# Which token tiles are gathered and which go through the dense expert pass: tiles 0, 3, 6, 7 against tiles 0, 5, 6, 7, with other token steps

## The chip, the cores and the metric

The kernel runs on one core of a Trainium2 chip. The metric is the device time of the whole program in microseconds (us), as the median of several runs. The kernel before takes 3573.17 us (three runs, 3567.7 to 3573.94). The execution that the profiler recorded took 3550.3 us, and its span, from the first to the last instruction, is 3548.6 us.

## What is computed

One decoder block over 1024 tokens of width 1024, in float32. Cut to what matters here:

```python
u = modulate(rmsnorm(x, norm_mix_g), sh_mix, sc_mix)
p = u @ w_in
mix = concat([conformer_conv(p[:, :1024]), rwkv7_mix(p[:, 1024:])]) @ w_out   # rwkv7: a scan over the tokens
x = x + gt_mix * mix
u = modulate(rmsnorm(x, norm_ffn_g), sh_ffn, sc_ffn)
# PEER: per token 8 heads, each with the best 16 of 128 x 128 experts
q = u @ w_q ; s = q . sub_keys ; best 16 of 256 candidates -> expert[t, h, k], gate = softmax(best)
h = gelu(sum_d expert_u[expert[t, h, k]] * u[t])
x = x + gt_ffn * sum_{h,k} gate * h * expert_v[expert[t, h, k]]
out = rmsnorm(x, final_g)
```

Each token uses 128 experts (8 heads, 16 each) of 16384. One expert is one row of `expert_u` and one of `expert_v`, 4 KB each.

## The kernel before

The 1024 tokens are eight tiles of 128. There are two ways to compute the experts of a tile.

- **Gathered** tiles (`GATHER`). For each of the tile's 128 selected experts per token, POOL issues one indirect DMA that brings, for all 128 tokens, the expert's row of u and v: 128 x 2048 floats, 1 MB, into one of three buffers `row` (`ROWS = 3`, `stream_fetch`). VectorE forms the dot product of the row's first half with the token (`stream_use`, result `hj`), ScalarE applies gelu and the gate to `hj`, and VectorE adds the second half, scaled by `hj`, to an accumulator (`stream_add`). Then the buffer is free for the next row. In the first stage a quarter of the dot products is done by POOL and ScalarE instead (`SHARE`, `stream_useg`), the operands lie in SBUF, and the accumulator is called `acc`; in the second stage the token copy `up` and the accumulator `ap` lie in PSUM.
- **Dense** tiles (all others, `DT_`). The selected experts and gates become two one-hot matrices per token (`onea`, `oneb`, `stream_g`), a matmul makes of them the token's 128 x 128 gate matrix, and this goes to DRAM (`Gd`, `stream_h`). Later one dense pass over all 16384 experts serves the four dense tiles at once (512 columns): 128 blocks of experts, each with 24 matmuls into `ph` and as many into `po`/`pC` (`stream_mm`), with loads of `w`, `v` and `gt`.

The program has two stages. In the first, these streams run side by side, each in its own order: `stream_a` (input projection, one step per entry of `MACROS`), `stream_l` and `stream_taps` (convolution), `stream_b` (the RWKV recurrence, tile after tile, strictly in sequence), `stream_c` (output projection, then the queries and the scores `s`, one step per entry of `MACROS`), `stream_d` (top 16, the selection and the gates), `stream_g` and `stream_h` (one-hots), and the gather streams. A step of `stream_c` starts its RWKV half when the recurrence has finished the last tile of the step, and `stream_d` releases a tile's experts after the scores of its whole step. The gathered tiles are fetched in the order of their numbers, one row after the other.

The first stage ends when the recurrence, the convolution and the one-hots of all dense tiles are done and `stream_c` has passed the output projection of the last step (line 1395). Then its memory is released and the second stage starts: the dense pass, the rest of `stream_c` and `stream_d`, and the gathers that are left. A tile's final norm (`tile_end`) follows its last row; the dense tiles are finished in `stream_sum`.

The order of the instructions of each engine is fixed when the program is built. A planner (`Issue.go`) picks, step by step, the operation of any stream that can start first by its own cost model. In it all transfers share one resource, and a gathered row takes 2920 ns of that (`GA`) while a 512 KB load takes 1456 ns (`LD`). On the chip each engine then follows that order and waits where an operand is late.

Lines that decide about the change:

```python
MACROS = [128, 128, 256, 256, 256]                                          # 65
GATHER = (0, 3, 6, 7)                                                       # 67
yield Wait(lambda: done["B"] >= i0 + nt - XB)                               # 572, stream_a, XB = 3
yield Wait(lambda: done["B"] >= i0 + nt)                                    # 981, stream_c
yield Wait(lambda: i in SEL and SEL[i].get("n", 0) > j)                     # 1260, stream_fetch
ROW[n] = tl(gat, [128, 2048], "row", bufs=ROWS)                             # 1261
```

Of the kernel before, what the change touches and what calls it, by code (L numbers as in the profile page):

```python
# [61 lines left out]
    _o += _w  # L62
NCOL = _o

MACROS = [128, 128, 256, 256, 256]

GATHER = (0, 3, 6, 7)
GE = 4
RUN_EXPERTS = True

# [212 lines left out]
def block_kernel(ctx, tc, xT, cols, ada_w, w_in, w0, w2a2, g2, w_out, w_q, keysT, peer_uv, peer_uT, outT, dbg=None):  # L283
# [5 lines left out]
    def LD(out, in_):  # L289
        nb = _free(out) * 4 * int(out.shape[0])  # L290
        return Op("SP", nc.sync.dma_start, (out, in_), {}, [out.name], [in_.name, out.name], 60, 0, dma=nb / 360.0)
# [20 lines left out]
    def tl(pool, shape, name, tag=None, bufs=1, dt=F32):  # L312
        return iss.tile(pool, shape, dt, name, tag or name, bufs)

    def pA():
        return tl(psum, [128, 512], "pA", bufs=PSA)
# [20 lines left out]

    NT = sum(MACROS) // 128
    GT_ = [i for i in range(NT) if i in GATHER]
    DT_ = [i for i in range(NT) if i not in GATHER]  # L340
    ND = len(DT_)
# [135 lines left out]
    def ada_dve(ns, wtag, ps_of, rowpool):  # L477
        for n in ns:
            row = tl(*rowpool)
            for k in range(KB):  # L480
                wt = tl(act if wtag == "A" else sel, [128, 512], "wt" + wtag, bufs=WB)
                yield LD(wt, ada_w[n, :, k])
                if k:
                    yield V.scalar_tensor_tensor(row, wt, sc_col[:, k:k + 1], row, op0=ALU.mult, op1=ALU.add)
                else:
                    yield A.activation(row, wt, AF.Copy, scale=sc_col[:, k:k + 1])
            p2 = ps_of()
            for j in range(4):
                yield PE.matmul(p2[:, j:j + 1], row[:, j * 128:(j + 1) * 128], ones1, start=True, stop=True)
            yield V.tensor_tensor(modc[:, n * 4:n * 4 + 4], p2[:, 0:4], cv("ada_b", n * 4, 4), op=ALU.add)  # L490
# [29 lines left out]
    def norm(x, n, pool, tag, ps, wide=None):  # L520
        if wide is not None:
            yield A.activation(wide, x, AF.Square)
        for k in range(KB):
            if wide is None:
                sq = tl(pool, [128, n], "sq" + tag)
                yield A.activation(sq, x[:, k, :], AF.Square)
            yield PE.matmul(ps[:, :n], onesD, sq if wide is None else wide[:, k, :], start=k == 0, stop=k == KB - 1)
        rs = tl(sel, [128, n], "rsC", tag="qT") if tag == "C" else tl(pool, [128, n], "rs" + tag)
        sq = tl(pool, [128, n], "sq" + tag)
        yield from rsqrt(rs, sq, ps[:, :n], RMS_EPS)  # L530
        kn = 1024 // n
        for k in range(0, KB, kn):
            yield V.tensor_tensor(x[:, k:k + kn, :], x[:, k:k + kn, :],
                                  rs.unsqueeze(1).to_broadcast([128, kn, n]), op=ALU.mult)
# [14 lines left out]
    def stream_a():  # L549

        u = tl(act, [128, 8, 256], "uA")[:, :, :MACROS[0]]
        yield LD(u, xT_v[:, :, 0:MACROS[0]])
        wide = tl(act, [128, 8, 128], "sqw", tag="xs", bufs=XB) if MACROS[0] == 128 else None
        yield from norm(u, MACROS[0], act, "A", pA(), wide)
        yield from ada_dve(range(4), "A", pA, (act, [128, 512], "adarow", "cb"))
# [4 lines left out]
        t0 = 0  # L560
        for n in MACROS:
            yield from macro_a(t0, n, u)
# [1056 lines left out]
```

## Time and profile before

| | |
|---|---|
| time, median of 3 runs | 3573.17 us |
| profiled execution | 3550.3 us |
| its span | 3548.6 us |
| PE busy | 3091.0 us, 87% |
| VectorE (DVE) busy | 2748.8 us, 77% |
| POOL busy | 2141.2 us, 60% |
| ScalarE (ACT) busy | 1580.8 us, 45% |
| moved by DMA | 923.00 MB, mean 260 GB/s |

The share of an engine is a mean over two stages with different limits, so the stages are read apart. A window of the trace gives, for one stretch, the busy time of each engine with its number of instructions, then the clock that TensorE was granted (1 is 2.4 GHz, 0.5 is 1.2 GHz), the busy share of the 16 DMA engines, and what they moved. Every helper records its operations under one line number (L220), so instructions are told apart by the names of their tiles.

### The profile page before, as it was taken

The page shows a single profiled execution, that of the slowest core. Times are in us where ns is not written, and L with a number is a line of the kernel's source. Part 1 is how long each engine was busy: PE and PEld are TensorE (multiplying, and loading weights), DVE is VectorE, ACT ScalarE, POOL GpSimd, SP SyncE. Part 2 cuts the span into 40 slices and gives each one's busy share as a digit, 9 for nine tenths or more (in the row PEclk, how much of TensorE's full clock was granted, in tenths as well). Part 3 has the DMA queues.
Part 4 walks back from the last instruction along what each step waited for, and adds up shares of the span by engine and source line. Part 5 has one row for each costly group of instructions (what it writes and reads, how often), then busy time and mean ns, then how long its engine had stood idle before and what let it go on. Part 6 is the DMA issues. An engine that isn't in the chain of part 4 may idle for free. (4 is left out here: it accounts for less than half of the span.)

```text
span 3548.6 us, 53713 instructions
## 1 busy us (share of the span) xinstructions
PE 3091.0 (87%) x18460; PEld 2530.7 (71%) x18460; DVE 2748.8 (77%) x5812; ACT 1580.8 (45%) x3843; POOL 2141.2 (60%) x2030
## 2 busy tenths in 40 slices
PE   4999998896899989686774688999999999999996
PEld 4788776775787767566673566777787777787774
DVE  5755987889869878898899887677777776677765
ACT  3445636537554534543675233333333333333332
POOL 0304657579854746667776877566666666666651
PEclk7799997897999988887887899999999999999998
DMA  6655776775678436666798578888898898899872
GB/s 201 212 185 168 280 273 212 266 263 189 207 267 291 151 105 224 226 208 216 264 293 313 201 275 295 308 327 318 334 342 326 325 332 314 324 335 341 333 278 83
DMA packets 356992, 923.00 MB, mean 260 GB/s; under 512 B 28912, under 2 KB 195952, under 8 KB 287216
## 3 DMA queue, kind: packets, MB, share of 16 engines
q0 software_dynamic: 73728, 536.90, 40.9%
q1 hardware_dynamic: 282992, 382.66, 32.5%
q8 instruction: 147, 2.41, 0.3%
q14 instruction: 125, 1.02, 0.1%
HBM read 873.33 MB, written 46.14 MB: 259 GB/s over the span
## 5 line engine op out<-in xcount | busy, mean ns | idle before, releaser
L220 POOL DMA_INDIRECT row<-in_peer_uv_dram,idx x512 | 550.6, 1075 | 487.0 <-DVE ap L220 186.4
L220 POOL TENSOR_TENSOR vl<-v,vh 128x512 fp32r<-128x512 f32 x256 | 335.4, 1319 | 185.3 <-ACT vh L220 183.4
L220 DVE SCALAR_TENSOR_TENSOR ap<-row,hj,ap 128x1024 f32<-128x1024 f32 x254 | 326.8, 1286 | 127.4 <-ACT hj L220 124.8
L220 DVE SCALAR_TENSOR_TENSOR acc<-row,hj,acc 128x1024 f32<-128x1024 f32 x250 | 381.4, 1526 | 52.5 <-ACT hj L220 50.7
L220 POOL TENSOR_TENSOR wl<-w,wh 128x1024 fp32r<-128x1024 f32 x128 | 309.0, 2414 | 133.3 <-ACT wh L220 128.6
L220 PE MATMUL pA<-uA,wtA 128*128 128x256 f32 (+1 forms) x1760 | 352.3, 352 | 11.7 <-ACT xs L220 4.8
L220 DVE CUSTOM_DVE_ANT_0 row<-row,up 128x1024 f32<-128x1024 f32 x258 | 313.3, 1214 | 49.2 <-DMA row<-in_peer_uv_dram,idx 48.7
L220 ACT ACTIVATE hj<-hj 128x1 f32<-128x1 f32 x512 | 101.3, 200 | 532.9 <-DVE hj L220 529.9
L220 POOL TENSOR_TENSOR cb<-cb,tap 128x256 f32<-128x256 f32 (+1 forms) x300 | 241.6, 806 | 149.4 <-ACT tap L220 131.9
L220 PEld LDWEIGHTS pA<-uA,wtA 128*128 128x128 f32 x1760 | 292.1, 200 | 48.7 <-ACT xs L220 5.3
L220 PE MATMUL ph<-uh,wh 128*128 128x512 f32 x1024 | 279.5, 419 | 49.4 <-ACT wh L220 43.1
L220 DVE CUSTOM_DVE_ANT_0 row<-row,u 128x1024 f32<-128x1024 f32 x190 | 277.0, 1459 | 43.3 <-DMA row<-in_peer_uv_dram,idx 43.3
L220 PE MATMUL pC<-uC,wtC 128*128 128x256 f32 (+1 forms) x1280 | 269.3, 366 | 12.6 <-ACT s L220 8.2
L220 PEld LDWEIGHTS ph<-uh,wh 128*128 128x128 f32 x1024 | 205.5, 204 | 102.8 <-ACT wh L220 43.3
L220 ACT CAST vh<-v 128x512 fp32r<-128x512 f32 x256 | 157.1, 619 | 269.6 <-PE pC L220 93.3
L220 PE MATMUL po<-ch,vh 128*128 128x512 f32 x512 | 208.5, 407 | 70.3 <-ACT ch L220 49.2
L220 PE MATMUL ph<-ul,wh 128*128 128x512 f32 x1024 | 258.6, 389 | 0.0
L220 PE MATMUL ph<-uh,wl 128*128 128x512 f32 x1024 | 256.6, 393 | 0.0
L220 PEld LDWEIGHTS pC<-uC,wtC 128*128 128x128 f32 x1280 | 223.0, 208 | 45.7 <-ACT s L220 9.9
L220 DVE TENSOR_TENSOR ph<-ph,gt 128x256 f32<-128x256 f32 x256 | 109.8, 429 | 150.3 <-ACT ph L220 147.8
L220 PEld LDWEIGHTS ph<-uh,wl 128*128 128x128 f32 x1024 | 196.0, 191 | 42.1
L220 PE MATMUL po<-ch,vl 128*128 128x512 f32 x512 | 208.0, 406 | 15.5 <-POOL vl L220 15.2
(323 smaller groups left out, 7461.9 us busy)
## 6 DMA issues: line engine op xcount, KB each, us to landing
v<-in_peer_uv_dram SPq DMA_DIRECT2D x128, 512.0 KB, 6.5
w<-in_peer_uT_dram SPq DMA_DIRECT2D x128, 512.0 KB, 5.4
wtA<-in_w_in_dram SPq DMA_DIRECT2D x220, 256.0 KB, 4.2
wtC<-in_w_q_dram SPq DMA_DIRECT2D x160, 256.0 KB, 4.7
gt<-Gd SPq DMA_DIRECT2D x31, 1024.0 KB, 8.7
wtC<-in_w_out_dram SPq DMA_DIRECT2D x80, 256.0 KB, 3.0
wtC<-in_ada_w_dram SPq DMA_DIRECT2D x64, 256.0 KB, 3.4
Gd<-stg SPq DMA_DIRECT2D x16, 1024.0 KB, 6.1
```

Source lines behind the costliest of these rows:

```text
L220: r = op.fn(*op.a, **op.k)
```

## The change

Two constants change. The dense tiles are then 1, 2, 3 and 4 and not 1, 2, 4 and 5; the steps of `stream_a`, `stream_l`, `stream_c` and `stream_d` are [0], [1, 2], [3, 4], [5, 6], [7] and not [0], [1], [2, 3], [4, 5], [6, 7]. The number of gathered and of dense tiles, of steps, and of rows is as before.

```diff
-MACROS = [128, 128, 256, 256, 256]
-
-GATHER = (0, 3, 6, 7)
+MACROS = [128, 256, 256, 256, 128]
+
+GATHER = (0, 5, 6, 7)
 GE = 4
 RUN_EXPERTS = True
```

## Rows read from the trace of the kernel before

**Rows 1.** Windows of all engines: us, busy by engine, clock, DMA share, GB/s
```profile
1320.00:1943.00 623.00, 461.06 (x3188) 384.40 (x3186) 544.61 (x1698) 341.98 (x794) 426.64 (x442) 0.80 0.74 252
1943.00:2188.00 245.00, 196.27 (x762) 152.69 (x763) 214.04 (x229) 80.54 (x177) 191.46 (x146) 0.90 0.69 242
2188.00:2823.00 635.00, 608.55 (x2593) 492.23 (x2592) 455.18 (x655) 231.94 (x527) 391.77 (x292) 0.98 0.88 326
```

**Rows 2.** The same windows, POOL's gathers alone: POOL busy (x rows issued)
```profile
339.00:1215.00 876.00, 153.97 (x128) 0.89 0.70 245
1215.00:1320.00 105.00, 0.00 (x0) 0.87 0.26 78
1320.00:1943.00 623.00, 107.65 (x91) 0.80 0.74 252
1943.00:2188.00 245.00, 45.01 (x38) 0.90 0.69 242
2188.00:2823.00 635.00, 121.97 (x128) 0.98 0.88 326
```

**Rows 3.** One of these windows, matmuls into ph alone (24 per block of experts)
```profile
2188.00:2823.00 635.00, 312.39 (x1287) 0.98 0.88 326
```

**Rows 4.** Timeline, four short stretches: second stage's first load, first matmul; last row, last dense matmul
```profile
1911.36 0.32 SPq L220 DMA_DIRECT2D accT<-u2T  x1
...
1943.11 1.22 PE L220 MATMUL ph<-uh,wh 128*128 128x512 f32 x2 [43.13 <-ACT wh L220]
...
3478.96 1.27 DVE L220 SCALAR_TENSOR_TENSOR acc<-row,hj,ap 128x1024 f32<-128x1024 f32 x1
...
3510.56 0.40 PE L220 MATMUL pC<-cl,vh 128*128 128x512 f32 x1
```

**Rows 5.** Timeline of DVE: last operations of the recurrence, tiles 2, 3, 5, 6, 7
```profile
626.02 0.85 DVE L220 SCALAR_TENSOR_TENSOR ym<-y,col,pB 128x128 f32<-128x128 f32 x3
...
866.75 0.59 DVE L220 SCALAR_TENSOR_TENSOR ym<-y,col,pB 128x128 f32<-128x128 f32 x2
...
1259.81 0.85 DVE L220 SCALAR_TENSOR_TENSOR ym<-y,col,pB 128x128 f32<-128x128 f32 x3
...
1450.22 0.33 DVE L220 SCALAR_TENSOR_TENSOR ym<-y,col,pB 128x128 f32<-128x128 f32 x1
...
1648.03 0.33 DVE L220 SCALAR_TENSOR_TENSOR ym<-y,col,pB 128x128 f32<-128x128 f32 x1
```

**Rows 6.** Windows, ScalarE's copies of scores (s) alone: steps [2, 3], [4, 5], [6, 7]
```profile
1015.00:1250.00 235.00, 5.85 (x16) 0.93 0.67 233
...
1365.00:1550.00 185.00, 5.92 (x16) 0.83 0.72 250
...
1740.00:1905.00 165.00, 6.01 (x16) 0.91 0.93 304
```

**Rows 7.** Windows, one-hots (readers of selT): DVE, ACT, POOL busy; tiles 1, 2, 4 and 5
```profile
799.00:1065.00 266.00, 50.46 (x110) 12.72 (x37) 69.20 (x62) 0.84 0.65 221
...
1364.00:1605.00 241.00, 38.64 (x124) 21.11 (x61) 71.51 (x72) 0.81 0.67 229
...
1687.00:1906.00 219.00, 88.75 (x272) 40.42 (x126) 103.67 (x116) 0.89 0.87 287
```

**Rows 8.** Page, part 5: the operations on a row (count | busy us, mean ns | idle before)
```profile
L220 DVE SCALAR_TENSOR_TENSOR ap<-row,hj,ap 128x1024 f32<-128x1024 f32 x254 | 326.8, 1286 | 127.4 <-ACT hj L220 124.8
L220 DVE SCALAR_TENSOR_TENSOR acc<-row,hj,acc 128x1024 f32<-128x1024 f32 x250 | 381.4, 1526 | 52.5 <-ACT hj L220 50.7
...
L220 DVE CUSTOM_DVE_ANT_0 row<-row,up 128x1024 f32<-128x1024 f32 x258 | 313.3, 1214 | 49.2 <-DMA row<-in_peer_uv_dram,idx 48.7
...
L220 DVE CUSTOM_DVE_ANT_0 row<-row,u 128x1024 f32<-128x1024 f32 x190 | 277.0, 1459 | 43.3 <-DMA row<-in_peer_uv_dram,idx 43.3
```

**Rows 9.** Page, part 3: the gather queue (packets, MB, share of 16 engines)
```profile
q0 software_dynamic: 73728, 536.90, 40.9%
```

**Rows 10.** Tile row, all 512 gathers: issue to landing
```profile
DMA to landing us min/median/max: 5.4/7.9/11.7
```

## Prediction

> **What bounds the kernel now.** I read the windows first, because the two stages have different limits, then the gathers alone, then the milestones of the streams.
>
> In the second stage PE is the engine that never rests: 608.55 of 635 us at a clock of 0.98, while VectorE is busy 455.18 us and POOL 391.77 us; the DMA engines are at 0.88 [rows 1]. In the same 635 us the gather brings 128 rows, 4.96 us each [rows 2], and 1287 matmuls go into ph, which is 53.6 blocks of experts at 24 each, 11.8 us a block [rows 3]. So 2.39 rows go by per block. The dense pass lasts from 1943 to 3511 us and the last row is added at 3479 to 3480 [rows 4]: both end within some 30 us of each other. The second stage is a race of two chains that now end together, and the one that is made longer sets the end.
>
> In the first stage nothing is saturated alone: VectorE is busy 544.61 of 623 us with PE at 461.06 us and a mean clock of 0.80 [rows 1]. The recurrence (tile 7 ends at 1648) runs ahead of the stage's end; the dense pass loads only at 1911 [rows 4, 5], right behind the one-hots of tiles 4 and 5, which are made from 1687 to 1906 [rows 7]. These one-hots hold the start of the dense pass.
>
> The gather has its own calendar: 128 rows of tile 0 from 339 to 1215, nothing for 105 us, then tile 3, of which 91 rows are issued before the dense pass starts at 1943 [rows 2]. Tiles 3, 6 and 7 are 384 rows; 91 of them are paid for in the first stage.
>
> **The change part by part.** Amounts of work stay: 512 rows, 128 blocks, four tiles of one-hots, five steps with the same weight loads. What moves is when each can begin.
>
> (1) The next gathered tile becomes 5. Its step [5, 6] needs the recurrence of tile 6, which ends at 1450 [rows 5]. From the end of the recurrence to the last score a step of two tiles took 1250 - 867 = 383 us for [2, 3], 1550 - 1260 = 290 us for [4, 5] and 1905 - 1648 = 257 us for [6, 7] (the windows' ends [rows 6] less [rows 5]). I take 290 us, the middle one and the one with a recurrence beside it as here: scores at 1740. The lookup of the experts adds some tens of us (for [2, 3]: first row at 1320 [rows 2], 70 us after the scores). Against this, VectorE loses the 91 rows of tile 3 that fell there, so I leave the recurrence where it is, take 60 us off and put 70 us on: **first row of tile 5 at 1750**. Ends: 1450 + 257 - 40 = 1667 and 1450 + 383 = 1833.
>
> What the rows cost VectorE there: a row in the first stage costs 1526 ns for the add and for three quarters 1459 ns for the dot product [rows 8], so 2.6 us, and 91 rows make 238 us of its 545 us of work from 1320 to 1943. This work leaves the stretch; it shortens the recurrence and the scores only where they stood behind it. The bounds are nothing and 238 us; tiles 6 and 7 of the recurrence took 1450 - 1260 = 190 and 1648 - 1450 = 198 us with rows beside them, which is no more than a tile takes anywhere (tile 3: 241) [rows 5], so I stay near the small end with the 60 us above.
>
> The Trainium skill has a rule that speaks for the change here. The page SBUF — State Buffer, section Who interferes with whom, says that a VectorE instruction with both inputs in SBUF competes with a reading GpSimd instruction for one port pair, and the later one blocks fully. The trace agrees in sign: add and dot product cost 1526 and 1459 ns with both inputs in SBUF, 1286 and 1214 ns with one in PSUM [rows 8]. By that, 128 rows moved to the second stage save VectorE another 128 x 0.42 = 54 us at most, and the end would come some 35 us earlier than I say; I put that into the range.
>
> (2) The dense tiles become 1 to 4. Tiles 1 and 2 now come in one step, behind the recurrence of tile 2 (627) and not 1, so their one-hots start near 627 + 383 = 1010, where tile 1's began at 799 [rows 5, 7]. One tile's one-hots took 266 and 241 us beside rows and recurrence, and 219 / 2 = 110 us at the end [rows 7]. In the new order the first has rows beside it, the next two the recurrence alone, the last little: 266 + 150 + 150 + 130 = 696, ready at 1706. The ends are 1010 + 266 + 3 x 110 = 1606 and 1010 + 266 + 3 x 241 = 1999.
>
> (3) The last step is one tile. stream_c reaches it after the scores of [5, 6] at 1740 and has the output projection of tile 7 to do, for which I allow 40 us: 1780. That is later than 1706, so it sets the end of the first stage, and the one-hots no longer do. Between the first load and the first matmul of the dense pass lie 32 us [rows 4]: **first dense matmul at 1815**, 128 us earlier than now. Queries and selection of tile 7 follow in the second stage, where now none of the matmuls of the queries is left; I put 20 us on the pass for them.
>
> (4) The dense pass: 3511 - 1943 = 1568 us now, plus 20: **it ends at 3400**, some 110 us earlier.
>
> (5) The rows. Three tiles, 384 rows, begin at 1750. In the first 245 us of the second stage 38 rows went by, 6.45 us each [rows 2], since the selection shares VectorE; I take that pace to 2060: 48 rows. From there to 3400 at 4.96 us: 270. That leaves **66 rows when the dense pass is over**. The 2.39 rows per block are built into the order of VectorE's and POOL's instructions, so they do not flow faster while PE works through the pass.
>
> (6) The rows after the pass. No row was gathered alone so far, so this is bounded: below by the transfers, 40.9% of 3548.6 us for 512 rows = 2.83 us each [rows 9]; above by the 4.96 us of the dense pass. Three buffers go round, each with landing (5.4 us at least), dot product 1.21, add 1.29 and some 1 us for gelu, gate and hand-overs [rows 8, 10]: 8.9 us, 3.0 us a row at best, and with the median landing of 7.9 us 3.8. I take 3.3: 66 x 3.3 = 218 us. The ends give 187 and 327 us.
>
> The Trainium skill (DMA: Bandwidth & Descriptors, section Anatomy of one DMA — SWDGE (gpsimd) path) gives 2.0 us plus the bytes at 436 GB/s for such a transfer, an estimate of 4.4 us for this 1 MB. The shortest landing here is 5.4 us [rows 10]; by the page's figure the tail would be some 20 us shorter.
>
> Sum: 3400 + 218 + 20 for the last tile's norm and store = 3638 us of span, against 3549: **+89 us**. The profiled execution lies 1.7 us above its span and 22.9 us below the median of the runs, so on the scale of the medians I say 3573 + 90 = **3663 us**.
>
> **The rivals.**
>
> - *The first stage shrinks more than the tail costs.* If the missing rows let the scores of [5, 6] come at the short end, first row at 1667 and first dense matmul at 1740, the pass ends at 3328; 48 rows by 1977, 272 more, 64 left, at 2.83 us 181: 3529 of span, 20 us faster. For it speaks that VectorE was busy 87% of that stretch; against it that the recurrence is a chain. Decision point: some 95 us earlier than I say for both milestones.
> - *The rows flow faster in the dense pass.* Rows take 2.83 / 4.96 = 0.57 of the DMA engines' 0.88 [rows 1, 2, 9]; with all 0.69 that the dense loads leave, a row would take 4.1 us: 48 + 327, 9 left, 30 us: 3400 + 30 + 20 = 3450, 99 us faster. It decides below 4.5 us a row. Against it speaks the order that the planner writes: at its prices 2.39 rows and a block's loads (512 KB each of w and v, 256 KB of gates) fill 2.39 x 2.92 + 2.5 x 1.456 = 10.6 us of its one transfer resource per block, nearly the 11.8 us that a block takes, and that order would be written the same way again.
> - *The one-hots stay the lock.* At 241 us for each tile they end at 1999, first dense matmul at 2031, the pass ends at 3600; rows from 1750 at 6.45 us until 2270, 81, then 268, and 35 are left: 3600 + 116 + 20 = 3736, +187 us.
> - *It cancels.* Both shifts meet within a few us: 3549 of span.
>
> **How the numbers follow.** Forecast 0.54, one-hots stay or the tail is dearer 0.18, a short first stage 0.13, faster rows 0.09, cancelled 0.06. A measurement of this kernel can tell about 0.2%, 7 us, from no change. So faster 0.22, same 0.06, slower 0.72. The forecast alone spans 3590 to 3730; to leave no more than 2 in 10 out the range runs from 3530 to 3765: half of the cases on the fast side (3529 and 3450 of span with 24 us are 3553 and 3474) lie in it, and on the slow side the one-hots' 3736 with 24 and little more.
>
> **What would show it.** Right: no row issued between about 1215 and 1750; the first matmul into ph near 1815; some 60 to 70 rows issued after the last dense matmul near 3400, at 3 to 4 us each, with PE idle. Wrong: a first row before 1670, fewer than 30 rows after the pass, or a pass that itself ends after 3500.

## The result, and the profile after

The changed kernel takes 3617.95 us (median of 4 runs, 3611.93 to 3622.12) against 3570.43 us for the kernel before on the same chip (4 runs, 3544.62 to 3573.94): ratio 1.0149, 95% interval 1.0108 to 1.0189, so **slower by 1.5%**. The forecast was 3663 us, slower by 90 us; the medians lie 47.5 us apart. The two profiled executions have spans of 3548.6 and 3610.2 us; the 61.6 us between them are what the traces must explain.

First the gathers alone (POOL's indirect DMAs, busy time and rows issued, then clock, DMA share, GB/s), to be held against [rows 2]:

```profile
378.00:1202.00 824.00, 150.72 (x128) 0.87 0.70 245
1202.00:1713.00 511.00, 0.00 (x0) 0.91 0.40 117
1713.00:1815.00 102.00, 14.02 (x13) 0.72 0.88 308
1815.00:2060.00 245.00, 47.45 (x41) 0.92 0.79 279
2060.00:3385.00 1325.00, 257.69 (x271) 0.98 0.89 326
3385.00:3595.00 210.00, 55.87 (x59) 0.52 0.88 312
```

The hole behind tile 0 was 105 us long and is now 511. From 2060 to 3385 a row takes 4.89 us, as before. The new line is the last one: 59 rows are issued behind the dense pass, where before there was none. The timeline at the same four places as [rows 4], and the recurrence of tiles 2, 6 and 7 and the last output projection (uC) beside [rows 5]:

```profile
1780.82 0.77 SPq L220 DMA_DIRECT2D accT<-u2T  x1
...
1814.96 0.79 PE L220 MATMUL ph<-uh,wh 128*128 128x512 f32 x1 [16.10 <-ACT wh L220]
...
3594.82 1.28 DVE L220 SCALAR_TENSOR_TENSOR acc<-row,hj,ap 128x1024 f32<-128x1024 f32 x1 [0.60 <-ACT hj L220]
...
3385.28 0.40 PE L220 MATMUL pC<-cl,vh 128*128 128x512 f32 x1
...
680.66 1.11 DVE L220 SCALAR_TENSOR_TENSOR ym<-y,col,pB 128x128 f32<-128x128 f32 x4
...
1421.44 0.59 DVE L220 SCALAR_TENSOR_TENSOR ym<-y,col,pB 128x128 f32<-128x128 f32 x2
...
1721.65 0.34 DVE L220 SCALAR_TENSOR_TENSOR uC<-pC,modc,uC 128x128 f32<-128x128 f32 x1
...
1577.86 0.33 DVE L220 SCALAR_TENSOR_TENSOR ym<-y,col,pB 128x128 f32<-128x128 f32 x1
```

The dense pass starts 128 us earlier (1943 to 1815), lasts 1570 us as against 1568, and the span ends 225 us behind its last matmul as against 38. That is -128 + 2 + 187 = +61, the whole difference. The last windows show who works there (PE, PEld, DVE, ACT, POOL, clock, DMA share, GB/s), and the waits from 3390 to 3590 show for what:

```profile
1320.00:1815.00 495.00, 413.23 (x3304) 357.25 (x3303) 380.46 (x1543) 257.71 (x489) 279.83 (x430) 0.87 0.51 160
2060.00:3385.00 1325.00, 1271.28 (x5466) 1031.66 (x5465) 975.88 (x1423) 498.74 (x1124) 815.85 (x611) 0.98 0.89 326
3385.00:3595.00 210.00, 5.32 (x11) 1.84 (x10) 156.89 (x196) 34.84 (x127) 58.82 (x61) 0.52 0.88 312
```
```profile
ACT hj L220 <- DVE hj L220: 165.3, 58, 6.9
POOL row L220 <- DVE ap L220: 131.9, 54, 7.1
```

In the tail PE does 5.32 us of work in 210. POOL waits for VectorE's add to free a row buffer, ScalarE for VectorE's dot product: the gather alone.

The one-hots (DVE, ACT, POOL busy), one window per dense tile, beside [rows 7], and the scores of step [5, 6] beside [rows 6]:

```profile
1206.00:1440.00 234.00, 45.42 (x162) 12.83 (x36) 59.70 (x76) 0.87 0.28 81
1440.00:1562.00 122.00, 50.39 (x189) 3.47 (x10) 43.87 (x62) 0.97 0.38 111
1562.00:1665.00 103.00, 41.09 (x160) 4.17 (x14) 59.22 (x79) 0.95 0.57 167
1665.00:1775.00 110.00, 43.18 (x133) 20.27 (x64) 39.61 (x48) 0.84 0.73 234
```
```profile
1555.00:1685.00 130.00, 6.17 (x16) 0.95 0.56 163
```

They begin at 1206, not near 1010, and are over at 1775, 54 us behind the last output projection and 6 us before the first load of the dense pass: they are still the lock of the first stage.

### The profile page after: what moved, and what is told of

Read it like the earlier page. It is cut to its first block, busy times and chain, and to the rows that moved or that the text cites. A ratio compares the mean times of both kernels' runs of the same rounds, so it can differ in the third digit from the quotient of the medians.

```text
span 3610.2 us, 53595 instructions
## 1 busy us (share of the span) xinstructions
PE 3054.2 (85%) x18460; PEld 2509.4 (70%) x18460; DVE 2722.6 (75%) x5964; ACT 1527.7 (42%) x3648; POOL 1977.0 (55%) x2010
## 5 line engine op out<-in xcount | busy, mean ns | idle before, releaser
L220 POOL DMA_INDIRECT row<-in_peer_uv_dram,idx x512 | 525.8, 1027 | 606.9 <-DVE ap L220 349.4
L220 DVE SCALAR_TENSOR_TENSOR ap<-row,hj,ap 128x1024 f32<-128x1024 f32 x344 | 442.5, 1286 | 159.2 <-ACT hj L220 155.4
L220 DVE CUSTOM_DVE_ANT_0 row<-row,up 128x1024 f32<-128x1024 f32 x348 | 422.7, 1215 | 105.8 <-DMA row<-in_peer_uv_dram,idx 104.7
L220 PE MATMUL pA<-uA,wtA 128*128 128x256 f32 (+1 forms) x1760 | 360.4, 358 | 12.0 <-ACT xs L220 7.0
L220 POOL TENSOR_TENSOR cb<-cb,tap 128x256 f32<-128x256 f32 (+1 forms) x300 | 249.0, 830 | 141.4 <-ACT tap L220 120.1
L220 DVE SCALAR_TENSOR_TENSOR acc<-row,hj,acc 128x1024 f32<-128x1024 f32 x160 | 249.3, 1558 | 48.1 <-ACT hj L220 47.3
L220 PE MATMUL pC<-ch,vh 128*128 128x512 f32 x512 | 202.6, 396 | 22.8 <-DVE accT L220 20.0
L220 PEld LDWEIGHTS ph<-ul,wh 128*128 128x128 f32 x1024 | 192.0, 188 | 39.8
L220 DVE CUSTOM_DVE_ANT_0 row<-row,u 128x1024 f32<-128x1024 f32 x122 | 186.3, 1527 | 35.1 <-DMA row<-in_peer_uv_dram,idx 34.9
```

What stands on the lines that cost most here:

```text
L220: r = op.fn(*op.a, **op.k)
```

## Experiments

In the diffs a minus is the changed kernel or, where it is said, the kernel before. Ratios are against the kernel before on the same chip.

**Each constant alone.**

```diff
 MACROS = [128, 256, 256, 256, 128]      # e1_steps_only
-GATHER = (0, 5, 6, 7)
+GATHER = (0, 3, 6, 7)

-MACROS = [128, 256, 256, 256, 128]      # e2_tiles_only
+MACROS = [128, 128, 256, 256, 256]
 GATHER = (0, 5, 6, 7)
```

> New steps [0], [1, 2], [3, 4], [5, 6], [7], but tiles 0, 3, 6, 7 gathered as before. Theory (the loss is the gather's empty calendar between tile 0 and tile 5): tile 3 is released with step [3, 4], rows from about 1350 us, some 75 of them before the dense pass; one-hots of tile 5 hold the first dense matmul until about 1860; pass ends near 3435, no rows are left behind it; span about 3475, 2% faster than before. Rival (the new pairing of the steps itself costs time): within 1% of the changed kernel, 3575 to 3640.

Measured: 3612.5 us, ratio 1.0139 (1.0105 to 1.0172). A miss. Its one-hots of tiles 4 and 5, and its first and last dense matmul:

```profile
1697.00:1822.00 125.00, 43.27 (x119) 16.74 (x53) 58.37 (x67) 0.83 0.83 269
1822.00:1903.00 81.00, 0.00 (x0) 0.00 (x0) 0.00 (x0) 0.69 0.83 287
1903.00:2012.00 109.00, 57.25 (x128) 23.41 (x73) 45.61 (x56) 0.66 0.71 229
```
```profile
2051.72 1.65 PE L220 MATMUL ph<-uh,wh 128*128 128x512 f32 x3 [41.28 <-DMA v<-in_peer_uv_dram]
...
3573.45 0.39 PE L220 MATMUL pC<-cl,vh 128*128 128x512 f32 x1
```

Tile 3's rows did start at 1377 and no row was left behind the pass, as the theory has it. But dense tile 5 shares its step with gathered tile 6; its experts were ready so late, beside the rows, that one-hots stood still for 81 us, and the pass started at 2052. The other chain came last.

> Old steps [0], [1], [2, 3], [4, 5], [6, 7], but tiles 0, 5, 6, 7 gathered as in the changed kernel. Theory: tile 5 is released with step [4, 5], rows from about 1600 us; first dense matmul near 1815; pass ends near 3420; about 30 rows are left, 100 us; span about 3540, equal to before. Rival (which tiles are gathered costs by itself, whenever they come): as the changed kernel, 3600 or more; rival (the steps cost): about 3475.

Measured: 3624.96 us, ratio 1.0150 (1.0121 to 1.0179). A miss in size, with the mechanism in place: rows of tile 5 from 1673 (not 1600), first dense matmul at 1872 (not 1815), 44 rows behind the pass (not 30), span 3630.7 (not 3540). That span is also what the rival said; the 44 rows behind the pass, where the kernel before has none, speak for the theory. Each constant alone costs as much as both together: the two don't add up, they decide which chain is late.

**The rows behind the pass.** 62 rows of the last gathered tile left out.

```diff
-            for j in range(128):
+            for j in range(66 if m == 3 else 128):
...
-                old, inp = acc, second and j < 127
+                old, inp = acc, second and j < rows - 1
```

> The changed kernel with only 66 of the 128 rows of its last gathered tile; 62 rows (fetch, dot product, add) are left out. Theory (the rows behind the dense pass are the whole loss, and PE's pass does not care for them): the pass ends at 3385 plus or minus 15 as in the changed kernel, the last row at about the same time, span about 3425. Rival (the last rows only fill time in which something else is late, such as the norms and stores of the last tiles): span over 3500.

Measured: 3408.8 us in a single run, span 3407.1. The pass ends at 3386 as in the changed kernel, the last add is at 3380, and 21 us later all is stored. 62 rows are worth 203 us, 3.3 us each. The theory holds: the tail is these rows and nothing else.

**What sets the pace of the rows in the pass.** First the price that I had named.

```diff
-                  [out.name], [idx.name, out.name], 1050, 0, dma=2920.0)
+                  [out.name], [idx.name, out.name], 1050, 0, dma=2300.0)
```

> The changed kernel, planner's price of a row's transfer 2300 ns in place of 2920, nothing else. Theory (2.4 rows per block of experts are written into the order by that price): some 2.8 to 2.9 rows per block, 4.1 to 4.3 us a row in the pass, 15 to 35 rows left, the pass up to 2% longer because the DMA engines fill up; span 3490 to 3560. Rival (landings and three buffers set the pace, not the order): a row still takes 4.8 to 5.0 us, 60 rows or more are left, span 3600 or more.

Measured: 3641.01 us, ratio 1.0198 (1.0158 to 1.0237).

```profile
2065.00:3416.00 1351.00, 261.05 (x273) 0.97 0.87 321
3416.00:3620.00 204.00, 54.05 (x57) 0.51 0.87 307
```

1351 / 273 = 4.95 us a row: the lower price does not raise the pace, and my reason for it falls. Next a fourth row buffer in the second stage, first in memory that the late tiles' norms use too (`uC`), then in memory of its own.

```diff
+        def fourth():
+            return bool(second) and st["c"] in iss.over and all(m in FIN for m in X1) and (not more or more[-1]())
...
-            return Wait(lambda: len(ring) < ROWS or ring[-ROWS]())
+            return Wait(lambda: len(ring) < ROWS or ring[-ROWS]() or fourth())
...
-                ROW[n] = tl(gat, [128, 2048], "row", bufs=ROWS)
+                if fourth():
+                    ROW[n] = tl(sel, [128, 2048], "row4", tag="uC")
+                    more.append(lambda n=n: n in USED)
+                else:
+                    ROW[n] = tl(gat, [128, 2048], "row", bufs=ROWS)
+                    ring.append(lambda n=n: n in USED)
```

> The changed kernel with a fourth row buffer in the second stage (in the memory of uC, free by then). Theory A (three buffers times the time from a row's issue to its release set the pace of 4.9 us in the pass): 4.1 to 4.5 us a row in the pass, up to 25 rows left behind it, the pass up to 3% longer since the DMA engines fill; span 3430 to 3510. Theory B (the planner's transfer price sets 2.4 rows per block): 4.9 us, 55 to 60 rows left, span 3585 to 3605, only the tail shorter.

Measured: 3882.58 us, ratio 1.0872 (1.0830 to 1.0915), far outside both. The windows of the gathers, before and in the stop, all engines in the stop, and the longest wait from 2640 to 3320:

```profile
2060.00:2680.00 620.00, 129.05 (x136) 0.99 0.94 348
2690.00:3280.00 590.00, 176.73 (x188) 0.56 0.94 346
```
```profile
2690.00:3280.00 590.00, 64.62 (x261) 50.20 (x261) 473.51 (x609) 113.82 (x407) 203.31 (x205) 0.56 0.94 346
```
```profile
PEld po L220 <- DVE x L220: 517.4, 2, 514.4
```

Until 2680 a row takes 4.56 us. Then PE stands for 514 us at the final norm of tile 5, whose data waits for the memory that the row buffer shares: its load is issued only at 3197, when most of the rows are through. That is my edit's fault and not the kernel's.

> The kernel before with the same fourth buffer. Both chains end together there, so faster rows alone give nothing: if theory A holds, the last row comes 100 us or more earlier than 3479, the pass still ends at 3510 to 3560, span 3540 to 3600. Rival (rows hold the end of the kernel before as well): span below 3500.

Measured (the same edit on the kernel before): 3525.32 us, ratio 0.9888 (0.9841 to 0.9934). The gathers of both kernels (the kernel before first; the last start is what to read), then the end of the rows in this run:

```profile
L220 POOL DMA_INDIRECT row<-in_peer_uv_dram,idx x512: 932/958/2924, 339.4 to 3441.0; - x171
L220 POOL DMA_INDIRECT row<-in_peer_uv_dram,idx x512: 932/952/2921, 336.8 to 3344.4; - x171
```
```profile
3439.86 0.60 PE L220 MATMUL pC<-ident,acc 128*128 128x128 f32 x4
...
3440.49 1.28 DVE L220 SCALAR_TENSOR_TENSOR acc<-row,hj,ap 128x1024 f32<-128x1024 f32 x1 [2.97 <-PE pC L220]
```

The last row is fetched at 3344 in place of 3441 and its dot product comes at 3356 in place of 3449: the rows are over some 95 us earlier, close to the 100 of theory A, at 4.53 us a row (255 from 2188 to 3344). Only the last add stands late, at 3440 in place of 3479. It waits not for its row but for PE: the accumulator of tile 7 takes the memory of tile 3's, which PE reads just before it (3478 in the kernel before). The pass still ends last, at 3481 in place of 3511, so the 95 us give nothing by themselves. The span of 3520.0 lies between the two ranges, since the pass gained 30 us, which neither had foreseen.

> The changed kernel with the fourth buffer and the planner's price of 2300 ns. If buffers and price both cap the rows per block (A and B together): 4.0 to 4.3 us a row, no rows left, span 3430 to 3480, below the run with the buffer alone. If the buffers alone cap it: within 10 us of the run with the buffer alone. If neither: 55 rows left, span 3590 or more.

Measured (changed kernel): 3538.37 us, ratio 0.9911 (0.9881 to 0.9940). 260 rows from 2060 to 3240, 4.54 us each, the same as with the buffer alone (4.56): the price does not raise the pace with four buffers either. PE stops here as well, from about 3300 to 3450 (8.94 us of work in 150), so the comparison of the spans with `e5_fourth_buffer` tells nothing; the pace does.

> The changed kernel with a fourth row buffer that nothing else uses in the second stage: the late tiles' final norm takes its 8 KB from the wtC buffers, so the stop of the dense pass seen with the shared memory is gone. Theory A (buffers times the turn of a row set the pace): 4.4 to 4.6 us a row in the pass, the pass unbroken and over at 3385 to 3415, 30 to 45 rows left at 2.9 to 3.0 us, span 3510 to 3545. Theory B (the order's price): 4.9 us, 55 rows or more left, span 3585 or more.

The edit beside that of `e5_fourth_buffer`: a late tile's norm takes four `wtC` buffers in place of `uC`, and `fourth()` loses its condition on the norms (`all(m in FIN for m in X1)`).

```diff
-            X1[m] = tl(sel, [128, 2, 8, 128], "x1", tag="uC")
+            X1[m] = q4 = [tl(sel, [128, 4, 128], "x1w", tag="wtC", bufs=WB) for _ in range(4)]
```

Measured: 3513.02 us, ratio **0.9865 (0.9819 to 0.9912)**, faster than both kernels.

```profile
2060.00:3368.00 1308.00, 273.21 (x288) 0.99 0.92 345
3368.00:3503.00 135.00, 37.76 (x40) 0.53 0.91 334
```

4.54 us a row, 40 rows behind the pass at 3.4 us each (not 2.9 to 3.0), no stop; the pass is over at 3368. So the number of buffers held the rows at 4.9 us, not the price. On the chip it shows as rows that land too late: from 2100 to 3300 VectorE waits for landings in the changed kernel, and in this run that line is gone. The matmuls into ph of the same stretch, the changed kernel first, give the rows per block of experts:

```profile
DVE row L220 <- DMA row<-in_peer_uv_dram,idx: 62.2, 62, 3.1
```
```profile
2100.00:3300.00 1200.00, 591.41 (x2462) 0.98 0.89 327
2100.00:3300.00 1200.00, 595.08 (x2531) 0.99 0.93 348
```

With 244 and 265 rows issued there, that is 2.38 rows per block with three buffers (2.38 at the lower price too) and 2.51 with four. The planner counts the buffers as well, so it may write another order with four of them. No run keeps the old order with four buffers; how much of the pace is the ring on the chip and how much the order is therefore open.

With four buffers at the old turn it would be 4.9 x 3/4 = 3.7 us, but 4.54 is reached. By an estimate from this window, rows at 3.7 us would move 1.05 MB / 3.7 us = 283 GB/s, and the dense loads 114 beside them (345 less 1.05 MB / 4.54 us): 397 GB/s, where the most that any stretch of some 90 us shows in any run is 360. The DMA engines are at 0.92 now: the next bound is close behind the first.

**Other calendars with the same parts.** A theory of two calendars (pass starts when the last dense tile is ready, rows must be fed without a gap) promised more from an own step for tile 5.

```diff
-MACROS = [128, 256, 256, 256, 128]      # e9_steps_5_alone; e11 adds the edits of e8
-GATHER = (0, 5, 6, 7)
+MACROS = [128, 256, 256, 128, 256]
+GATHER = (0, 3, 6, 7)

-MACROS = [128, 128, 256, 256, 256]      # e10_steps_4_5_alone, from the kernel before
+MACROS = [128, 128, 256, 128, 128, 256]
```

> Tiles 0, 3, 6, 7 gathered as before, steps [0], [1, 2], [3, 4], [5], [6, 7], nothing else. Theory (two calendars: the pass starts when the last dense tile's one-hots are made, and the rows must be fed without a gap): tile 3's rows from about 1380 us; dense tile 5 is released with its own step near 1470, its one-hots are made by about 1790, first dense matmul near 1830, the pass ends near 3410, rows are over by then; span 3435 to 3490, faster than both kernels. Rival (steps that differ from the old ones cost time by themselves, or tile 5's one-hots still come last): 3570 or more, like the steps-only run.

Measured: 3589.98 us, ratio 1.0087 (1.0061 to 1.0114), span 3595.9. A miss; the rival's range.

> Tiles 0, 3, 6, 7 gathered as before, the old steps with [4, 5] cut in two: [0], [1], [2, 3], [4], [5], [6, 7]. One step more, so the weights of one step are loaded once more (14.5 MB). Theory: tile 4 is released near 1300 and tile 5 near 1480 where both came at 1560 to 1690; one-hots over near 1790 in place of 1900, first dense matmul near 1840 in place of 1943, pass-bound: span 3440 to 3500. Rival (the added step takes what the earlier release gives): 3530 to 3570.

Measured: 3563.79 us, ratio 1.0010 (0.9978 to 1.0043). The rival.

> The run with step [5] alone plus the fourth row buffer of its own. Theory: the pass sets the end there already, so faster rows give only what the pass gains from an earlier end of the rows, 10 to 40 us as in the kernel before with a fourth buffer: span 3410 to 3470. Rival (rows still hold the end there): 60 us or more below the run without the buffer.

Measured: 3525.9 us, ratio 0.9900 (0.9860 to 0.9940), 64 us below the run without the buffer: the rival's number, and a miss for the theory. The pass itself ends at 3492 in place of 3542, and no row is left behind it.

What these calendars have in common stands in one table, read from the traces: rows issued before the first dense matmul, that matmul, the last dense matmul, rows issued behind it, span.

| kernel | rows before | first dense matmul | pass ends | rows behind | span |
|---|---|---|---|---|---|
| changed kernel | 141 | 1815 | 3385 | 59 | 3610.2 |
| e2, tiles only | 158 | 1872 | 3456 | 44 | 3630.7 |
| e9, [5] alone | 196 | 1938 | 3542 | 7 | 3595.9 |
| before | 219 | 1943 | 3511 | 0 | 3548.6 |
| e10, [4] and [5] alone | 228 | 1994 | 3538 | 0 | 3561.0 |
| e1, steps only | 229 | 2052 | 3573 | 0 | 3596.3 |

The more rows lie in the first stage, the later it ends. The table alone does not say which is the cause: a stage that lasts longer also takes in more rows. But it shows that the releases planned for `e9_steps_5_alone` and `e10_steps_4_5_alone` did not bring the pass forward, and I had counted with the release only.

**What a row costs in the first stage.** The kernel before, with 1 of tile 3's 128 rows.

> The kernel before with 1 of the 128 rows of tile 3; 127 rows (fetch, dot product, add) are left out, and nothing else is released earlier or later. In the kernel before 91 of them lie in front of the first dense matmul at 1943. Theory (the early start of the dense pass in the changed kernel, 1815, comes from the missing rows, which cost the first stage about 1.6 us each): first dense matmul at 1790 to 1830. Rival (it comes from the earlier release of the last dense tiles, as the prediction had it): it stays at 1900 to 1945, since tiles 4 and 5 are released as late as before. In between: both.

Measured: 3438.92 us in a single run. The end of the recurrence, and the first dense matmul (this kernel's helper has line 221):

```profile
1598.74 1.11 DVE L221 SCALAR_TENSOR_TENSOR ym<-y,col,pB 128x128 f32<-128x128 f32 x4
```
```profile
1868.68 2.92 PE L221 MATMUL ph<-uh,wh 128*128 128x512 f32 x6 [43.39 <-ACT wh L221]
```

134 rows are issued before that matmul in place of 219, and it comes at 1869 in place of 1943: 74 us for 85 rows, 0.87 us each. The recurrence ends 49 us earlier. So of the changed kernel's 128 us, some 68 (78 rows fewer at 0.87 us) answer to the missing rows by this price, and 60 are left for the earlier release: both, and neither theory alone. This split is an estimate. No run takes the release alone, the first dense matmul comes at 1815 to 1827 in four runs with the same first stage, and the price is that of one calendar: from steps only to the changed kernel, which differ in the gathered tiles alone, 88 rows and 237 us go.

## Why the prediction was right, step by step

- **Both chains end within some 30 us in the kernel before: the rows end earlier.** I read their end from the last add at 3479, but that add waits for PE, as the run of the kernel before with the fourth buffer shows. The last dot product is at 3449, 62 us before the pass ends. The sum did not use the 30 us.
- **First row of tile 5, 1750: it was 1713.** The recurrence of tile 6 ended at 1421, 29 us earlier than I had left it, and the step's scores took 259 us (the last one is copied at 1680), not 290: together the 60 us that I had taken off. The first row came 33 us behind the scores, not 70. The bound of 1667 held.
- **One-hots over at 1706, and no longer the lock: this step failed.** They ended at 1775 and stayed the lock. The single times were near (234, 122, 103, 110 us against 266, 150, 150, 130), but they began at 1206 and not at 1010: with 256 columns in step [1, 2] the recurrence of tile 2 ended at 681 and not 627 (681 to 682 in the three kernels with this step, 615 to 636 in the four that have tile 1 alone), and the selection of two tiles at once lasted from the scores' end near 1045 to 1206. The output projection that I had put in their place was over at 1722, not 1780. The two errors met: first load 1780.8, first dense matmul 1815, to the microsecond where I had it, for a reason that was half wrong. That hit is luck.
- **The share of the missing rows.** I let the missing rows work on the first row alone and said that the start of the pass moves by the release. By the run without tile 3's rows they are about half of it.
- **The pass, 1568 + 20 and an end at 3400:** 1570, end 3385. The 20 us for the queries of tile 7 were not needed.
- **Rows in the pass, 48 + 270, 66 left:** 54 by 2060, 271 after it, 59 left. The pace was right (4.89 us). **Its reason was wrong**: not the planner's price, which leaves the pace as it is, but the number of buffers, as four buffers at the same price show. The rival "faster rows" named the bound that the rows meet then, the DMA engines, but not the pace: 4.54 us, not 4.1.
- **The tail, 66 x 3.3 = 218 us:** 59 rows, 210 us from the last matmul to the last add, 3.6 us each. Then 14 us to the end, not 20. Once the last work of the dense tiles was done, the lone rows went by at 3.33 us (51 from 3420 to 3590), as I had taken; the mean is dearer by the start, 8 rows in the first 35 us.
- **The sum, 3638 of span: 3610.2.** The 28 us are 15 from the end of the pass, 8 from the tail and 5 to 6 from the last norm and store; they all go one way, and the step that failed does not show in them because two errors cancelled in it.
- **The median.** The difference of the medians is 47.5 us, that of the profiled executions 61.6. The changed kernel's profiled execution is the fastest of its four runs; I had carried one offset of 23 us over to both.

For the rule on the shared port pair (the Trainium skill, SBUF — State Buffer, section Who interferes with whom) I had said that the trace agrees in sign. In the means it does again: adds with both inputs in SBUF cost 1558 ns (160 of them), those with one in PSUM 1286 (344). But the medians are alike, 1283 and 1287 ns (1278 and 1289 in the kernel before); the means differ by some long ones, up to 5970 ns, and no run here shows what made those long. It did not decide anything, since the dearer adds went away and the end came later all the same.

## What to carry to other kernels

When two chains end together, price the same piece of work by the place where it lies: here a row costs some 0.87 us of the first stage, little in the dense pass (it lasts 1546 us with 251 rows, 1568 with 293, 1570 with 312), and 3.3 us behind it. Moving work out of a crowded stage pays only while the cover of the next stage lasts; count what is left when that cover ends. Read the end of a chain from its own work: the last add of the kernel before stood 30 us behind its row, waiting for something else. And a pace that looks like an order or a bandwidth may be a ring of buffers: pace times the number of buffers is the turn of one buffer, and one more buffer tells at once (4.9 to 4.54 us a row here; 1.1% off the kernel before, and the changed kernel with it is 1.35% below that one). It also shortened the dense pass, by 29 to 49 us in the three pairs of runs that it did not stop; why was not taken apart.

## What had not been expected

Rows alone and rows beside the dense loads come to the same rate with four buffers: 346 GB/s with the pass at rest, 348 with PE at work, at 0.94 of the DMA engines' time. The pages of the runs, which cut each span into 40 slices of some 90 us, show 360 at most (the run with the fourth buffer and the lower price, from 3181 to 3270). The Trainium skill (DMA: Bandwidth & Descriptors, section Specifications) gives about 358 GB/s as the HBM limit per core, half of what a stack gives two cores. The rates come close to it, and one slice lies above it; but this kernel runs on one core, and no run shows that this limit is the one that holds the rows. Why four buffers stop at 345 GB/s and 4.54 us and not a little lower was not taken apart further, nor were the fourth buffer and a later start of tile 5's rows tuned together; 40 rows are still behind the pass in the fastest kernel.
